# The down projection of a decoder layer by seven quarter products, with weight sums made by accumulating transfers

## The chip, the cores and the metric

The kernel runs on one core of one Trainium2 chip. A core has five engines that run side by side, each through its own list of instructions in order: TensorE (PE; its weight loads are listed as PEld), VectorE (DVE), ScalarE (ACT), GpSimd (POOL) and SyncE (SP, which here only issues transfers). Sixteen DMA engines move data between the main memory (HBM) and the on-chip memory SBUF; matmul results go to PSUM, from which DVE and ACT read them. The metric is the time of one execution on the device in microseconds (us), as the median of the runs shown. Engines wait for one another through semaphores that a framework places, from the order in which the program names the operations and from the tiles that they read and write.

## The reference

One decoder layer: two parallel token mixers (gated linear attention and sliding-window attention with sinks), merged by gates, an output projection, a layer norm, then a SwiGLU channel mixer and a second norm. There is one sequence of 512 tokens, a model width of 1024 and a channel-mixer width of 2816, all in float32. What matters here is the end:

```
def swiglu_ffn(h, w_gate, w_up, w_down):
    return (jax.nn.silu(h @ w_gate) * (h @ w_up)) @ w_down
...
        h = layer_norm(DEEPNORM_ALPHA * h + mix, ln1_g[layer], ln1_b[layer])
        ffn = swiglu_ffn(h, w_ffn_gate[layer], w_ffn_up[layer], w_ffn_down[layer])
        h = layer_norm(DEEPNORM_ALPHA * h + ffn, ln2_g[layer], ln2_b[layer])
```

The down projection is the product of the activations (512 x 2816) and `w_down` (2816 x 1024).

## The kernel before

A float32 product is made of three products of a reduced format (float32r). Every operand is split into a high part, which is the value cast to float32r, and a low part, which is the value minus the high part. High x high, low x high and high x low are then added up in one PSUM bank of 128 x 512. So each product of two tiles is three matmuls, and each operand costs a cast on ACT and a subtraction on DVE or POOL.

The weights are streamed. `plan` (L103) lists units of 128 x 1024 floats (512 KB); `fetch_to` (L141) has SP load them into three rotating buffers `raw`; `prep_to` (L149) casts a unit on ACT to `wh` (L161) and subtracts on DVE to `wl` (L162), five rotating buffers of each; `weight` (L166) hands out the parts and prepares three units ahead of use. `feat_tile` (L222) multiplies one 128-column weight tile with the whole of a transposed activation, 24 matmuls for eight k-tiles (L230).

The stages follow in the order of the text: the input projections with both mixers woven in between, branch products and gates (from L672), the merge, the output projection with tokens on partitions (L756 for the first half of the columns, L767 for the second), the first norm (`norm_part` L713, `norm_end` L718), a transposition (`transpose_in` L206), SwiGLU (from L773), the down projection (from L800) and the second norm. In SwiGLU each of 22 feature tiles f takes a gate product, an up product and `swiglu` (L776): a sigmoid on ACT (L778), two multiplications on DVE (L779, L780), then the split of the activation, a cast to `ah` on ACT (L783) and a subtraction to `al` on POOL (L784).

The down projection holds 22 k-tiles of `ah` and `al` and streams `w_down` in 22 units. The first 512 columns are finished for all four token tiles in four PSUM banks, then the second 512. For the last eight k-tiles of the second half the loop goes by token tile, so that the norm of one token tile runs beside the matmuls of the next; the last token tile is cut into two halves of 256 columns. `down` (L803) issues the three matmuls (L807). `norm_part` adds the residual and takes statistics (L715, L716). `norm_end` centres on DVE (L727), refines the root and then scales and shifts, either on DVE (L739) or, for the columns that `aside` names, on ACT (L742) and POOL (L743). SP and ACT store the two halves of each row (L834, L835).

Residual tiles and the gains of the norms are loaded from POOL's queue (L710, L704). All of SBUF's tiles come from one pool: 44 rotating tiles `hold`, 12 `scratch`, two `big` ones for the transposed activations, and the weights' buffers. PSUM has four banks `mm` and four `at`. A scheduler sets each engine's list from the program's order and from when it expects operands to be ready; `tc.issue_after` puts an instruction behind a named one.

## Time and profile before

| what | value |
|---|---|
| runs | 878.52, 881.78 and 878.04 us; median 878.52 |
| the profiled execution's span | 876.6 us, mean clock 0.995; its own time has 1.9 us more, if it stood at the median |
| PE busy | 854.8 us of the span |
| DVE, ACT, POOL busy | 448.8, 319.7, 127.3 us |
| moved by DMA | 83.03 MB, 95 GB/s in the mean |
| the down projection, from SwiGLU's last matmul to its own last | about 746 to 867 us of the span |

The head of the page gives each engine's busy time; its slices cut the span into forty parts and give the busy share of each part in tenths, with the clock that PE was granted. The groups of instructions give, for one line, engine and shape, how many there were, their busy time, the mean length of one in ns, and the idle time ahead of them with what ended it. The chain of waits follows the work that ended last back to its releasers (start, length, engine, tile, line, number). The order of time lists single instructions with start and length. A table of stretches gives, for a window, its length, the busy time of PE, PEld, DVE, ACT and POOL with the number of their instructions, then PE's clock, the share of the DMA engines and GB/s.

### The profile page before, as it was taken

The numbers are of one execution on the slowest core, as the hardware profiler recorded it, in microseconds if no ns is written. First come the engines' busy times: TensorE is split into PE (matmuls) and PEld (weight loads), VectorE is DVE, ScalarE is ACT, GpSimd is POOL, SyncE is SP. The second block draws the span as 40 slices with busy tenths as digits, with TensorE's granted clock in tenths as the row PEclk, the third lists the DMA queues.
The fourth block names the chain that finished last, engine by engine and source line by source line (L and its number), as shares of the span: only waits on it lengthen the run. The fifth ranks groups of instructions, "written<-read, shape, count | busy, mean of one in ns | idle before, by whom it ended". The sixth has DMA issues, their size and how long they took to land.

```text
span 876.6 us, 10823 instructions
## 1 busy us (share of the span) xinstructions
PE 854.8 (98%) x4226; PEld 710.2 (81%) x4226; DVE 448.8 (51%) x850; ACT 319.7 (36%) x570; POOL 127.3 (15%) x126
## 2 busy tenths in 40 slices
PE   6999999999999999999998999999999999999995
PEld 6887777777887888888887898888888888888885
DVE  4898887686676533322454854333333333224227
ACT  4557566464543431122343133333332222211111
POOL 3240220112310230000231001111111111000001
PEclk9999999999999999999999999999999999999998
DMA  8423113122122223322228103333333332322402
GB/s 241 145 72 96 49 49 97 49 72 74 49 74 71 96 96 96 96 95 97 96 91 293 49 9 113 96 96 97 97 96 97 100 99 98 125 100 79 143 0 97
DMA packets 69443, 83.03 MB, mean 95 GB/s; under 512 B 4128, under 2 KB 56368, under 8 KB 69392
## 3 DMA queue, kind: packets, MB, share of 16 engines
q1 hardware_dynamic: 67248, 76.88, 27.5%
q0 software_dynamic: 1568, 4.40, 1.5%
q10 hardware_dynamic: 576, 1.05, 0.3%
q8 instruction: 33, 0.54, 0.2%
q14 instruction: 18, 0.15, 0.1%
HBM read 80.23 MB, written 2.10 MB: 94 GB/s over the span
## 4 chain that ended last, share of the span: by engine, by line
PE 83%; issue 13%; DMA 2%; POOL 1%; ACT 0%; DVE 0%; SPq 0%; POOLq 0%; ACTq 0%; DVEq 0%
PE pg L230 12%; PE pu L230 12%; PE pva L424 5%; PE pq L230 5%; PE pr L230 5%; PE pgb L230 5%; PE pbb L230 5%; PE pba L230 5%; PE pga L230 5%; PE pw L767 3%; PE pka L230 3%; PE pqa L230 2%; PE pw L756 2%; PE po L405 2%; PE pp L394 2%
## 5 line engine op out<-in xcount | busy, mean ns | idle before, releaser
L162 DVE TENSOR_TENSOR wl<-raw,wh 128x1024 fp32r<-128x1024 f32 (+1 forms) x144 | 176.7, 1231 | 216.7 <-ACT wh L161 216.2
L161 ACT CAST wh<-raw 128x1024 fp32r<-128x1024 f32 (+1 forms) x144 | 147.1, 1027 | 236.2 <-PE pdn L807 74.8
L807 PE MATMUL pdn<-wh,al 128*128 128x512 f32 (+1 forms) x198 | 72.5, 366 | 0.0
L807 PE MATMUL pdn<-wh,ah 128*128 128x512 f32 (+1 forms) x198 | 72.4, 366 | 0.0
L807 PE MATMUL pdn<-wl,ah 128*128 128x512 f32 (+1 forms) x198 | 71.9, 365 | 0.0
L784 POOL TENSOR_TENSOR al<-sg,ah 128x512 fp32r<-128x512 f32 x22 | 33.2, 1509 | 249.1 <-ACT ah L783 249.1
L230 PE MATMUL pg<-h1h,wh 128*128 128x512 f32 x160 | 62.3, 389 | 0.0
L230 PE MATMUL pg<-h1l,wh 128*128 128x512 f32 x160 | 62.3, 389 | 0.0
L230 PE MATMUL pg<-h1h,wl 128*128 128x512 f32 x160 | 62.2, 389 | 0.0
L230 PE MATMUL pu<-h1h,wh 128*128 128x512 f32 x160 | 62.2, 389 | 0.0
L230 PE MATMUL pu<-h1l,wh 128*128 128x512 f32 x160 | 62.2, 389 | 0.0
L230 PE MATMUL pu<-h1h,wl 128*128 128x512 f32 x160 | 62.2, 389 | 0.0
L807 PEld LDWEIGHTS pdn<-wh,ah 128*128 128x128 f32 x198 | 37.4, 189 | 6.3
L807 PEld LDWEIGHTS pdn<-wh,al 128*128 128x128 f32 x198 | 37.4, 189 | 6.1
L807 PEld LDWEIGHTS pdn<-wl,ah 128*128 128x128 f32 x198 | 37.3, 188 | 6.1
L780 DVE TENSOR_TENSOR sg<-pu,sg 128x512 f32<-128x512 f32 x20 | 13.8, 692 | 46.8 <-PE pu L230 46.8
L230 PEld LDWEIGHTS pg<-h1l,wh 128*128 128x128 f32 x160 | 30.1, 188 | 6.3
L230 PEld LDWEIGHTS pg<-h1h,wl 128*128 128x128 f32 x160 | 30.1, 188 | 6.3
L230 PEld LDWEIGHTS pu<-h1h,wl 128*128 128x128 f32 x160 | 30.0, 188 | 6.3
L230 PEld LDWEIGHTS pu<-h1l,wh 128*128 128x128 f32 x160 | 30.0, 188 | 6.2
L230 PEld LDWEIGHTS pu<-h1h,wh 128*128 128x128 f32 x160 | 30.1, 188 | 6.1
L230 PEld LDWEIGHTS pg<-h1h,wh 128*128 128x128 f32 x160 | 30.0, 188 | 6.1
(423 smaller groups left out, 1942.3 us busy)
## 6 DMA issues: line engine op xcount, KB each, us to landing
raw<-in_w_in_dram SPq DMA_DIRECT2D x50, 512.0 KB, 3.4
raw<-in_w_ffn_gate_dram SPq DMA_DIRECT2D x22, 512.0 KB, 3.5
raw<-in_w_ffn_up_dram SPq DMA_DIRECT2D x22, 512.0 KB, 3.5
raw<-in_w_ffn_down_dram SPq DMA_DIRECT2D x22, 512.0 KB, 3.2
raw<-in_w_branch_b_dram SPq DMA_DIRECT2D x8, 512.0 KB, 3.3
raw<-in_w_branch_a_dram SPq DMA_DIRECT2D x8, 512.0 KB, 3.4
raw<-in_w_out_dram SPq DMA_DIRECT2D x8, 512.0 KB, 3.2
x<-in_x_dram SPq DMA_DIRECT2D x8, 256.0 KB, 6.6
```

Of the source, the lines that this page charges most:

```text
L161: ACT.copy(wh, src)
L162: DVE.tensor_tensor(wl, src, wh.bitcast(F32), ALU.subtract)
L230: PE.matmul(ps[:, n0:n1], w, d[k][:, n0:n1] if isinstance(d, list) else d[:, k, n0:n1], start=i == 0, stop=i == 3 * NK - 1)
L394: PE.transpose(pt[:, h * P : (h + 1) * P], S[h][:, n * P : (n + 1) * P], ident)
L405: PE.matmul(po[par * HD : (par + 1) * HD, 0:2, :], vtok[:, blk * P + kv * HD : blk * P + (kv + 1) * HD], PT[n][:, par::2, :], start=n == 0 ...
L424: PE.matmul(pa[c], d[:, k, cs], w, start=k == 0 and i == 0, stop=k == NK - 1 and i == 2)
L756: PE.matmul(pw[t], d[k][:, ts], w, start=k == 0 and i == 0, stop=k == NK - 1 and i == 2)
L767: PE.matmul(ps, d[k][:, ts], w, start=n == 0, stop=n == 3 * NK - 1)
L780: DVE.tensor_tensor(sg, pu, sg, ALU.mult)
L784: POOL.tensor_tensor(tl, sg, th.bitcast(F32), ALU.subtract)
L807: PE.matmul(ps[:, c0:c1], d[k][:, ts], w[:, c0:c1], start=start and n == 0, stop=stop and n == 2)
```

## The change

Both operands of the down projection are cut into quarters: the activations into A11, A12 (tokens 0 to 255, first and second eleven k-tiles) and A21, A22 (tokens 256 to 511), the weights into B11, B12 (first eleven k-tiles; first and second 512 columns) and B21, B22. The eight quarter products are replaced by seven products of quarters and of sums of quarters:

| product | PSUM | left operand | right operand |
|---|---|---|---|
| 1 | X | A11 | B11 |
| 2 | Y | S1 = A21 - A22 | T1 = B11 + B12 |
| 3 | X, added to | S2 = S1 - A11 | T2 = T1 + B22 |
| 4 | W | A22 | T4 = T2 + B21 |
| 5 | Z | A12 | B21 |
| 6 | X, added to | A11 - A21 | T3 = B12 + B22 |
| 7 | Y, added to | S4 = A12 + S2 | B22 |

Products 2, 3 and 4 are interleaved by pairs of k-tiles, each a step behind the one before. Each of X, Y, W and Z is two banks, for two token tiles. As partial results are complete, DVE adds or subtracts them into the residual tiles.

The sums of the activations are made by DVE, pair by pair, in tiles `ssum`. The sums of the weights are made in the `raw` tiles by transfers that add to what they find there, issued from POOL's queue. The activations are kept in float32 after SwiGLU and are split when a product needs them. The weights of this stage are no longer in `plan` and are split by a function of their own.

The one SBUF pool becomes several that follow each other in the same memory: `xparts` (then `merged`, then `operands`) on one side, `early` and `mix` (then `late`, with `h1` and then `sums` behind it) on the other. A tile of a new pool waits for the users of the tiles that lay there. The residual and gain tiles, the second half of the output weights and the activations lie in `late`; the output weights' second half is split in whole units of 1024 columns.

The diff, cut to its core (the pools' renamings and the unchanged parts are left out):

```
-    for j in range(2):
-        plan(("dn", j), rows(w_ffn_down[0], 0, NF, 512 * j))
...
-                parts = [(hold(f"wh{i}_{n}", F32R), hold(f"wl{i}_{n}", F32R), raw[:, 512 * n : 512 * n + 512])
-                         for n in range(2)]
+                parts = [(four(f"wh{i}", F32R), four(f"wl{i}", F32R), raw)]
...
+    right.release()
+    right = phase("merged", "right")
...
+    mix.release()
+    early.release()
+    late = phase("late")
...
     def swiglu(f, pg, pu):
+        a = act[f // HF][f % HF // 2][:, f % HF % 2, :]
         sg = scratch(f"sg{f}")
         ACT.activation(sg, pg, AF.Sigmoid)
         DVE.tensor_tensor(sg, pg, sg, ALU.mult)
-        DVE.tensor_tensor(sg, pu, sg, ALU.mult)
-        new = hold if f < 18 else scratch
-        th, tl = new(f"ah{f}", F32R), new(f"al{f}", F32R)
-        ACT.copy(th, sg)
-        POOL.tensor_tensor(tl, sg, th.bitcast(F32), ALU.subtract)
-        ah.append(th)
-        al.append(tl)
+        DVE.tensor_tensor(a, pu, sg, ALU.mult)
...
+    def load(name, p, src):
+        home, bufs = (wpool, NRAW) if name in ("b11", "b21") else (top, 7)
+        raw = home.tile([P, 1024], F32, tag="raw", name=f"raw{name}{p}", bufs=bufs)
+        nc.sync.dma_start(raw.rearrange("p (k c) -> p k c", c=512)[:, : n_of(p)], src)
+        return raw
+
+    def add(raw, p, src):
+        nc.gpsimd.dma_start(raw.rearrange("p (k c) -> p k c", c=512)[:, : n_of(p)], src, accum_op=ALU.add)
+
+    def split_w(name, p, raw):
+        n = 512 * n_of(p)
+        wh, wl = [wpool.tile([P, 1024], F32R, tag=t, name=f"{t}{name}{p}", bufs=5) for t in ("wh", "wl")]
+        ACT.copy(wh[:, :n], raw[:, :n])
+        DVE.tensor_tensor(wl[:, :n], raw[:, :n], wh[:, :n].bitcast(F32), ALU.subtract)
+        return wh, wl
+
+    def split_a(name, p, src):
+        op = right.tile([P, 2, 2, 256], F32R, tag="op", name=f"op{name}{p}", bufs=8)
+        n = n_of(p)
+        ACT.copy(op[:, 0, :n], src[:, :n])
+        POOL.tensor_tensor(op[:, 1, :n], src[:, :n], op[:, 0, :n].bitcast(F32), ALU.subtract)
+        return op
...
+    def terms(ps, op, w, p, t, start, stop, c0=0, c1=512):
+        todo = [(j, x, y) for j in range(n_of(p)) for x, y in ((0, 0), (1, 0), (0, 1))]
+        for i, (j, x, y) in enumerate(todo):
+            PE.matmul(ps[:, c0:c1], op[:, x, j, t * P : (t + 1) * P], w[y][:, 512 * j + c0 : 512 * j + c1],
+                      start=start and i == 0, stop=stop and i == len(todo) - 1, skip_group_check=True)
...
+    b11 = [load("b11", p, quarter(0, 0, p)) for p in range(3)]
+    traw = {}
+    for p in range(NP_):
+        if p >= NP_ - 3:
+            q = p - (NP_ - 3)
+            traw[q] = load("t", q, quarter(0, 0, q))
+            if q >= 1:
+                add(traw[q - 1], q - 1, quarter(0, 1, q - 1))
+        if p + 3 < NP_:
+            b11.append(load("b11", p + 3, quarter(0, 0, p + 3)))
+        both(X, op_a11(p), split_w("b11", p, b11[p]), p, p == 0, p == last)
...
+    for s in range(NP_ + 2):
+        if s + 3 < NP_:
+            traw[s + 3] = load("t", s + 3, quarter(0, 0, s + 3))
+        if 2 <= s + 2 < NP_:
+            add(traw[s + 2], s + 2, quarter(0, 1, s + 2))
+        if s >= NP_ - 1:
+            q = s - (NP_ - 1)
+            b21[q] = load("b21", q, quarter(1, 0, q))
+        if s < NP_:
+            w1, o1 = split_w("t1", s, traw[s]), op_s1(s)
+            add(traw[s], s, quarter(1, 1, s))
+            both(Y, o1, w1, s, s == 0, s == last)
+        if 0 <= s - 1 < NP_:
+            p = s - 1
+            w2, o2 = split_w("t2", p, traw[p]), op_s2(p)
+            add(traw[p], p, quarter(1, 0, p))
+            both(X, o2, w2, p, False, p == last)
+        if 0 <= s - 2 < NP_:
+            p = s - 2
+            both(W, op_a22(p), split_w("t4", p, traw[p]), p, p == 0, p == last)
...
+    for p in range(NP_):
+        if p + 3 < NP_:
+            b21[p + 3] = load("b21", p + 3, quarter(1, 0, p + 3))
+        if p >= 1:
+            t3[p - 1] = load("t3", p - 1, quarter(0, 1, p - 1))
+        if p >= 2:
+            add(t3[p - 2], p - 2, quarter(1, 1, p - 2))
+        both(Z, op_a12(p), split_w("b21", p, b21[p]), p, p == 0, p == last)
...
+    for p in range(NP_):
+        if p + 5 < NP_:
+            t3[p + 5] = load("t3", p + 5, quarter(0, 1, p + 5))
+        if p + 4 < NP_:
+            add(t3[p + 4], p + 4, quarter(1, 1, p + 4))
+        if p >= 2:
+            b22[p - 2] = load("b22", p - 2, quarter(1, 1, p - 2))
+        both(X, op_s3(p), split_w("t3", p, t3[p]), p, False, p == last)
...
+    for p in range(4, NP_):
+        b22[p] = load("b22", p, quarter(1, 1, p))
+    early_ = 2
+    for p in range(early_):
+        both(Y, op_s4(p), split_w("b22", p, b22[p]), p, False, False)
+    ops = [op_s4(p) for p in range(early_, NP_)]
+    ws = [split_w("b22", p, b22[p]) for p in range(early_, NP_)]
+    for t in range(2):
+        norm_end(2 + t, st2[2 + t][:, 0:2, :], g2, b2, "b", (512, 512))
+        store(2 + t)
+    scaled = None
+    for t in range(2):
+        spans = [(0, 512)] if t == 0 else [(0, 256), (256, 512)]
+        for n, (c0, c1) in enumerate(spans):
+            for p in range(early_, NP_):
+                terms(Y[t], ops[p - early_], ws[p - early_], p, t, False, p == last, c0, c1)
+            with tc.issue_after(scaled.ins) if n else nullcontext():
+                norm_part(Y[t], t, 1, st2[t], 1 + n, c0, c1, first=False)
+        scaled = norm_end(t, st2[t][:, 0 : 1 + len(spans), :], g2, b2, "b", (0, 0) if t == 0 else (256, 0), t == 1)
+        store(t)
```

A quarter has eleven k-tiles, so six pairs p, the last with one tile (`n_of`). `both` calls `terms` for the two token tiles of a half.

More of the change, by code (lines that the diff above doesn't have):

```diff
@@ L698, in tile_decoder_layer, with two, scratch @@
             ml.append(tl)
+    mix.release()
+    early.release()
+    late = phase("late")
+    def two(name, tag, bufs, dt=F32):
+        return late.tile([P, 512], dt, tag=tag, name=name, bufs=bufs)
+    def scratch(name, dt=F32):
+        return two(name, "scratch", 4, dt)
     def vec_bcast(v, name):
-        ts = [hold(f"{name}{i}") for i in range(2)]
+        ts = [two(f"{name}{i}", "gain", 4) for i in range(2)]
         for i in range(2):
@@ L705, in vec_bcast @@
         return ts
-    res = [[hold(f"res{t}_{i}") for i in range(2)] for t in range(NT)]
+    res = [[two(f"res{t}_{i}", "res", 8) for i in range(2)] for t in range(NT)]
     for t in range(NT):
@@ L798, in tile_decoder_layer @@
         swiglu(f, pg, pu)
+    right.release()
+    right = phase("operands", "right")
+    top.release()
+    top = phase("sums")
+    ssum = [top.tile([P, 2, 256], F32, tag=f"ssum{p}", name=f"ssum{p}") for p in range(NP_)]
     g2, b2 = vec_bcast(ln2_g, "g2"), vec_bcast(ln2_b, "b2")
     st2 = new_stats("b")
-    def down(k, t, ps, w, start, stop, c0=0, c1=512):
-        ts = slice(t * P, (t + 1) * P)
-        h, l = w
-        for n, (d, w) in enumerate(((ah, h), (al, h), (ah, l))):
-            PE.matmul(ps[:, c0:c1], d[k][:, ts], w[:, c0:c1], start=start and n == 0, stop=stop and n == 2)
@@ L824, in tile_decoder_layer @@
-    last = [weight(("dn", 1), k, 0, 512) for k in range(split, NF)]
-    aside = [(0, 0), (0, 0), (512, 512), (256, 0)]
-    scaled = None
-    for t in range(NT):
-        for n, (ps, span) in enumerate(zip(pw[t], spans[t])):
-            for k in range(split, NF):
-                down(k, t, ps, last[k - split], False, k == NF - 1, *span)
-            with tc.issue_after(scaled.ins) if n else nullcontext():
-                norm_part(ps, t, 1, st2[t], 1 + n, *span)
-        scaled = norm_end(t, st2[t][:, 0 : 1 + len(spans[t]), :], g2, b2, "b", aside[t], t == NT - 1)
+    wd_rows = w_ffn_down[0].rearrange("(k p) c -> p k c", p=P)
@@ new lines, in tile_decoder_layer @@
+    last = NP_ - 1
+    b11 = [load("b11", p, quarter(0, 0, p)) for p in range(3)]
[10 more added lines that the diff above has]
+    for t in range(2):
+        r = res[t][0]
+        DVE.scalar_tensor_tensor(r, r, ALPHA, X[t], ALU.mult, ALU.add)
@@ new lines, in tile_decoder_layer @@
+    for t in range(2):
+        r = res[t][1]
+        DVE.scalar_tensor_tensor(r, r, ALPHA, X[t], ALU.mult, ALU.subtract)
+        for i, ps in ((0, W), (1, Y)):
+            r = res[2 + t][i]
+            DVE.scalar_tensor_tensor(r, r, ALPHA, ps[t], ALU.mult, ALU.add)
+    for p in range(NP_):
[6 more added lines that the diff above has]
+        both(Z, op_a12(p), split_w("b21", p, b21[p]), p, p == 0, p == last)
```

109 lines of the change are left out of this document (77 added, 32 removed).

## The prediction, made before the change was run

> **What bounds the kernel now.** I read the head of the page first, then its slices.
>
> ```profile
> span 876.6 us, 10823 instructions
> PE 854.8 (98%) x4226; PEld 710.2 (81%) x4226; DVE 448.8 (51%) x850; ACT 319.7 (36%) x570; POOL 127.3 (15%) x126
> PE   6999999999999999999998999999999999999995
> PEclk9999999999999999999999999999999999999998
> DMA  8423113122122223322228103333333332322402
> GB/s 241 145 72 96 49 49 97 49 72 74 49 74 71 96 96 96 96 95 97 96 91 293 49 9 113 96 96 97 97 96 97 100 99 98 125 100 79 143 0 97
> ```
>
> PE is busy 98% of the span at full clock, and every other engine has half its time free. The last six slices (21.9 us each) hold the down projection: PE nines until the end, DMA at four tenths or less. So only fewer matmuls, or a shorter head or tail, can gain. A busy PE is not yet PE at its pitch; the chain of waits gives that, and a table of stretches says whether the down projection has the same.
>
> ```profile
> 735.53 5.44 PE pg L230 x24
> 749.72 61.68 issue
> 752.00:792.00 40.00, 40.00 (x178) 33.15 (x177) 9.75 (x8) 8.43 (x8) 0.00 (x0) 1.00 0.27 92
> ```
>
> 24 matmuls in 5.44 us are 0.2267 us each; 178 in the 40 us of the down projection (both ends cut into one) agree. The columns after PE and its loads are DVE, ACT and POOL: there they work 24%, 21% and 0%, and the DMA engines 27%. (The chain itself shows the down projection as "issue", because it follows a gain load on POOL; so I cost this stage from PE's own rows.) The profiled execution spans 876.6 us, the median of the runs is 878.52: 1.9 us lie around the span, and I add them at the end.
>
> **What is removed.** The down projection is 22 k-tiles x 4 token tiles x 2 column halves x 3 terms = 528 matmuls of 512 columns. Seven products of 11 k-tiles x 2 token tiles x 3 terms are 462. Shapes and operand types stay, so the pitch stays: 66 x 0.2267 = 15.0 us less, and 462 x 0.2267 = 104.7 us left. A product is 15.0 us, one pair of k-tiles of one product 12 x 0.2267 = 2.72 us. That is all the change can win here; the rest is what it pays. In pairs of k-tiles a product is 5.5, seven are 38.5.
>
> **What is added on ACT, DVE and POOL.** Before, the weights of this stage were split in 22 units, and the activations in 22 inside SwiGLU. After, each of 38.5 pairs needs a weight split (ACT cast, DVE subtraction) and an activation split (ACT cast, POOL subtraction), and four operand sums of 5.5 pairs need a DVE add. Rows with these shapes, from the page and from the groups of instructions:
>
> ```profile
> L161 ACT CAST wh<-raw 128x1024 fp32r<-128x1024 f32 x136 | 142.8, 1051 | 229.6 <-PE pdn L807 74.8 <-PE pbb L230 34.2 <-PE pg L230 28.2
> L783 ACT CAST ah<-sg 128x512 fp32r<-128x512 f32 x22 | 13.6, 619 | 58.0 <-DVE sg L780 57.8 <-issue 0.2
> L693 DVE TENSOR_TENSOR gb<-gb,ga 128x512 f32<-128x512 f32 x8 | 5.5, 692 | 0.3
> L784 POOL TENSOR_TENSOR al<-sg,ah 128x512 fp32r<-128x512 f32 x22 | 33.2, 1509 | 249.1 <-ACT ah L783 249.1
> L727 DVE SCALAR_TENSOR_TENSOR res<-res,mva,g 128x512 f32<-128x512 f32 x8 | 5.9, 747 | 0.1
> L743 POOL TENSOR_TENSOR res<-res,b 128x512 f32<-128x512 f32 x2 | 2.5, 1258 | 53.3 <-ACT res L742 53.3
> ```
>
> ACT: 38.5 x (1.05 + 0.62) = 64.3 us of 104.7, covered. The casts that leave SwiGLU gain nothing: PE bounds that stage too. DVE and POOL are another matter, since POOL's 1509 ns is a mean of two cases, which the order of time shows (start, length):
>
> ```profile
> 551.51 1.23 DVE L162 TENSOR_TENSOR wl<-raw,wh 128x1024 fp32r<-128x1024 f32 x1 [0.21 <-ACT wh L161]
> 552.07 1.81 POOL L784 TENSOR_TENSOR al<-sg,ah 128x512 fp32r<-128x512 f32 x1 [9.58 <-ACT ah L783]
> 606.48 1.29 POOL L784 TENSOR_TENSOR al<-sg,ah 128x512 fp32r<-128x512 f32 x1 [9.08 <-ACT ah L783]
> 529.43 3.45 DVE L162 TENSOR_TENSOR wl<-raw,wh 128x1024 fp32r<-128x1024 f32 x2
> 530.39 1.40 POOL L784 TENSOR_TENSOR al<-sg,ah 128x512 fp32r<-128x512 f32 x1 [1.55 <-ACT ah L783]
> ```
>
> Alone POOL's subtraction takes 1.29 us. Started inside a DVE subtraction it takes 1.81 and ends 1.14 us after DVE's end (553.88 against 552.74). The other way round, two DVE subtractions with a POOL one between them take 3.45 us, and the second ends 1.09 us after POOL's (532.88 against 531.79). They take turns: a weight split and an activation split cost 1.09 + 1.14 = 2.23 us of one shared thing. For 38.5 pairs that is 85.9 us; the 22 sums at 0.69 add 15.2; the norms of token tiles 2 and 3, which fall into the last product, 4 x 0.75 on DVE and 4 x 1.26 on POOL, 8.0. Together 109.1 us against 104.7 of PE: 4.4 us over. What is done before the first matmul of the stage counts against it; the first product uses activations that are complete halfway through SwiGLU. One pair ahead is certain (2.2 us), three are likely (6.7, by the five buffers of split weights). I take one: 2.2 us lost, between nothing and 4.4. (DVE alone has 38.5 x 1.23, the 15.2, the 3.0 and 24 readings of a PSUM bank or a row of statistics at about the same 0.69: 82 us, covered.)
>
> The Trainium skill (SBUF — State Buffer, Who interferes with whom) says that a VectorE instruction with two SBUF inputs and a GpSimd instruction that reads SBUF exclude each other, the later one waiting for the whole of the earlier. The trace agrees in kind; by whole instructions the sum would be larger, which is the second rival.
>
> **What is added in transfers.** Loads: B11, the running sum's first quarter, B21, T3's first, B22: 27.5 units of 512 KB, in place of 22 units that moved the whole matrix once. Accumulating transfers: three into each of the six running sums, one into each of six T3 tiles, 24 in all, 22 units. The rows for their price:
>
> ```profile
> q1 hardware_dynamic: 67248, 76.88, 27.5%
> q0 software_dynamic: 1568, 4.40, 1.5%
> raw<-in_w_ffn_down_dram SPq DMA_DIRECT2D x22, 512.0 KB, 3.2
> res<-in_x_dram POOLq DMA_DIRECT2D x8, 256.0 KB, 7.4
> L710 POOL DMA_DIRECT2D res<-in_x_dram x8 | 4.3, 552 | 0.0
> ```
>
> 76.88 MB in 27.5% of 876.6 us of sixteen engines are 319 GB/s when busy, 1.64 us for 512 KB; POOL's queue has 335 GB/s by its row. No transfer before accumulates. Its price lies between a plain one, 1.64 us, and two, 3.28 us, since the tile is read as well as the weights; a gain is excluded, since the same bytes still arrive. I take the middle, 2.4, as it is near neither end for a reason. The Trainium skill (DMA: Bandwidth & Descriptors, Where 436 GB/s comes from) puts the ceiling at 435 GB/s; two reads of 512 KB would be 2.4 us by that, an estimate; no row here shows it.
>
> The middle of the stage is three interleaved products (Y, X, W), in steps of 3 x 2.72 = 8.16 us. A step issues one load and three accumulations: 1.64 + 3 x 2.4 = 8.84 us, 0.68 over, 3.7 us in 5.5 steps (with cheap accumulations 6.6 us: hidden). Counted over the five products after the first but the last one (74.8 us): 20.5 loads and 22 accumulations less the three and two issued in the first product, 76.7 us, 1.9 over. I take 3.7. The fence's last row gives POOL 0.55 us per issue, 13.2 us for 24: with 38.5 x 1.29 = 49.7 POOL is occupied 63 us of 104.7.
>
> **Queues behind the new waits.** POOL issues in order, so an accumulation that waits for a load holds the activation splits behind it. In the first product the earliest waits for a tile that lies where SwiGLU's inputs did: free at SwiGLU's end, landing 3.2 us later. The splits behind it, for pairs four and five, are due 4 x 2.72 = 10.9 us after that end: covered. In the middle each accumulation follows the split of the same tile and is read a step, 8.16 us, later; even 7.4 us to landing, which the eight issued together had, fits. If that cover is gone, each microsecond over shows once as a shift, and PE's idle time has a second price:
>
> ```profile
> 475.56 1.05 ACT wh L161
> 476.00:478.60 2.60, 0.00 (x0) 0.03 (x1) 2.48 (x4) 1.39 (x2) 0.00 (x0) 1.00 0.75 241
> 478.60:482.00 3.40, 3.40 (x9) 2.65 (x10) 3.40 (x6) 2.16 (x3) 0.00 (x0) 0.53 0.77 239
> ```
>
> After 2.6 us without a matmul, at the output projection, the clock was 0.53 for 3.4 us: 9 matmuls where 15 fit, another 1.4 us. Short waits spread over the steps, as I expect, keep clear of this.
>
> **Pools in phases.** The memory of a phase serves the next, tile by tile. The residual and the second half of the output weights land where branch operands lay that the merge reads last, and are needed one output half, 8 x 4 x 3 x 0.2267 = 21.8 us, later. Hidden; if not, the 2.6 us gap above grows or, as the weights come in one cast of 1.05 instead of two of 0.62, shrinks. I put it at 0, between -2 and +3.
>
> **The tail.**
>
> ```profile
> 860.04 1.41 DVE L739 SCALAR_TENSOR_TENSOR res<-res,yb,b 128x512 f32<-128x512 f32 x2
> 867.25 0.42 DVE L715 SCALAR_TENSOR_TENSOR res<-res,pdn 128x256 f32<-128x256 f32 x1 [1.23 <-PE pdn L807]
> ```
>
> Before, DVE stood idle 1.23 us for PE's last matmul, because the tile before the last left its scale and shift to ACT and POOL. Now that tile keeps them on DVE (1.41 us, the first row's pair), and its successor's matmuls are 21, not 24 (0.7 us less cover). 1.41 + 0.7 - 1.23 = 0.9 late at most, nothing if the scale and shift are put behind the last tile's statistics; I take 0.7, since the order written has them ahead.
>
> **Sum:** 876.6 - 15.0 + 3.7 + 2.2 + 0 + 0.7 = 868.2 us of span, 870.1 with what lies around it.
>
> **Rivals.** (1) The accumulations are dear. For: nothing before does them, they read what they write. Against: the DMA engines are at 27% in this stage, and the plain price leaves 13 us to spare. At 3.28 us the middle needs 20.5 x 1.64 + 22 x 3.28 - 3 x 1.64 - 2 x 3.28 = 94.3 us against 74.8: 19.5 us late, 876.6 - 15.0 + 19.5 + 0.7 + 1.9 = 883.7, slower; at 3.5 us 888. It decides from 3.0 us per 512 KB, where its delay is the 14.3 us that are won.
> (2) DVE and POOL bound the stage by turns of whole instructions: 38.5 x (1.23 + 1.29) + 15.2 + 8 = 120.2 us, 15.5 over, 8.8 to 13.3 after one to three pairs ahead; with 11, 876.6 - 15.0 + 11 + 0.7 + 1.9 = 875.2, no change to speak of. For: any wait on a cast or a landing leaves the turn unused. Against: the two turns measured above are shorter than the rows' lengths. This is the rule of the skill's page named above, taken at its word.
> (3) The new pools hold up the output projection or SwiGLU's start, by 3 us or more of waiting and clock, with the rest as forecast: 874 to 877.
>
> **How the numbers follow.** Forecast 0.55, at 864 to 874; rival 1 0.21, rival 2 0.17, rival 3 0.07. A measurement of this kernel tells 0.5%, 4.4 us, from no change: faster is below 874.1, slower above 882.9. Faster: the forecast and a little of rival 3, 0.57. Slower: rival 1 and little else, 0.22. The rest, 0.21, lies between. Range: nothing lost, 876.6 - 15.0 + 1.9 = 863.5, is the low end; the high end is 886, within rival 1, beyond which about 0.12 lies. The forecast's own range is 864 to 874.
>
> **What would show it.** Right: 462 matmuls in the down projection at 0.2267 us, gaps of under a microsecond before pairs of the middle, DVE and POOL subtractions end on end, accumulations of 2 to 3 us of sixteen engines. Rival 1: ACT's casts there wait for POOL's transfers, the DMA row at nines, the clock dipping. Rival 2: PE waits on POOL's splits with the DMA engines half idle. Rival 3: PE's gaps before SwiGLU. Wrong altogether: PE's pitch changed, or a tail over 11 us.

## The result and the profile after

| | before | after |
|---|---|---|
| median of four runs | 879.0 us (878.04 to 881.78) | 906.59 us (904.05 to 909.47) |
| span of the profiled execution | 876.6 us | 902.3 us |
| the down projection, from its first matmul's start to its last one's end | 121.0 us | 137.0 us |
| the tail, from PE's last matmul to the end | 9.43 us | 14.36 us |

The change makes the kernel slower: ratio 1.0316, 95% interval 1.0285 to 1.0347. The forecast was 870.1 us, the range ended at 886. First the head of the page after, with its slices (22.6 us each):

```profile
span 902.3 us, 10790 instructions
PE 857.2 (95%) x4115; PEld 699.6 (78%) x4115; DVE 515.9 (57%) x896; ACT 345.4 (38%) x608; POOL 188.7 (21%) x172
PE   7999999999999999999999999999999999497993
PEclk9999999999999999999999999999999999799997
DMA  8423113131222223333356133333333338999532
```

PE's row of nines, unbroken before, has a 4 and a 7 in the down projection. With the 4 the clock falls to 7 tenths, and the DMA row stands at 8 and 9 for four slices, where it had 2 to 4. 25.7 us of span are to be found: 4.7 are gone before SwiGLU (its first matmul starts at 508.6 us, before at 503.9), 16.0 in the down projection, 4.9 in the tail.

In the down projection 462 matmuls are left, as predicted, but PE waits and then runs slowly. The waits of the profile after, from 745 to 890 us: engine, tile and line, what it waited for, then total, times and longest.

```profile
ACT wht L858 <- DMA rawt<-in_w_ffn_down_dram: 31.9, 10, 7.1
...
PE dny L879 <- DVE wlt L859: 6.2, 1, 6.2
...
PE dnx L879 <- ACT wht L858: 5.1, 1, 5.1
PE dnw L879 <- ACT wht L858: 4.5, 2, 2.5
```

PE waits for split weights, and the casts that make them wait for transfers. PE's gaps in this stage are 19.6 us. Around them the clock is at half in four stretches, 20.5 us in all. Of these 5.2 us lie in the gaps themselves; the other 15.3 us do half the work, so 7.6 us are lost to the clock. The stretch with the two longest gaps, in the table of stretches (39 matmuls in 26 us at a clock of 0.74, DMA engines at 0.95):

```profile
766.00:792.00 26.00, 13.36 (x39) 9.68 (x38) 15.81 (x13) 6.89 (x8) 15.53 (x14) 0.74 0.95 188
```

The transfers that add, by the groups and the issues of the page after:

```profile
L853 POOL DMA_DIRECT2D rawt<-in_w_ffn_down_dram x24 | 30.7, 1361 | 21.0 <-DMA rawt<-in_w_ffn_down_dram 12.5
...
rawt<-in_w_ffn_down_dram POOLq DMA_DIRECT2D x20, 512.0 KB, 9.2
```

And their queue from 750 to 880 us (packets, MB, share of sixteen engines):

```profile
q0 software_dynamic: 6016, 11.54, 50.7%
```

0.507 x 130 us are 65.9 us of sixteen engines for 22 units: 3.0 us for 512 KB, where 2.4 was forecast, and 9.2 us from issue to landing. A packet of 2 KB takes 184 ns; plain ones on SP's queue take 100. POOL needs 1.36 us to issue one, not 0.55.

The pitch changed too. Two groups of the chain of waits:

```profile
277.00 5.60 PE pgb L233 x24
840.02 10.98 PE dnz L879 x47
```

5.60 us for 24 matmuls are 0.2333 each (before: 5.47 in the same place, 0.228), and 10.98 for 47 are 0.2336. SwiGLU kept 0.2267. For 462 matmuls the longer pitch is 3.0 us. Together, -15.0 + 19.6 + 7.6 + 3.0 = 15.2 us, an estimate from these numbers, accounts for most of the 16.0 us that the stage is longer. Last, the tail: DVE in order of time around PE's last matmul, which ends at 888.0:

```profile
887.06 1.23 DVE L501 TENSOR_TENSOR yb<-yb,wb 128x1 f32<-128x1 f32 x1
890.33 0.41 DVE L740 TENSOR_TENSOR res<-res,dny 128x256 f32<-128x256 f32 x1
890.66 2.16 DVE L764 SCALAR_TENSOR_TENSOR res<-res,yb,b 128x512 f32<-128x512 f32 x2
892.75 0.41 DVE L741 BATCH_NORM_STATS2 bnb<-res 128x6 f32<-128x256 f32 x1
```

DVE takes the last sum 2.3 us after PE's end, because norms of earlier tiles are still in its list (an operation on one column, 0.15 us elsewhere, takes 1.23 here), and puts the scale and shift of tile 0 ahead of the last statistics, as the prediction read it from the order.

### The profile page after: what moved, and what is told of

Same layout as the page of the kernel before. It is cut to its first block, busy times and chain, and to the rows that moved or that the text cites. A ratio compares the mean times of both kernels' runs of the same rounds, so it can differ in the third digit from the quotient of the medians.

```text
span 902.3 us, 10790 instructions
## 1 busy us (share of the span) xinstructions
PE 857.2 (95%) x4115; PEld 699.6 (78%) x4115; DVE 515.9 (57%) x896; ACT 345.4 (38%) x608; POOL 188.7 (21%) x172
## 4 chain that ended last, share of the span: by engine, by line
PE 84%; DMA 7%; POOL 3%; issue 2%; DVE 2%; ACT 1%; SPq 0%; POOLq 0%; ACTq 0%; DVEq 0%
PE pg L233 12%; PE pu L233 12%; PE pgb L233 5%; PE pva L427 5%; PE pq L233 5%; PE pga L233 5%; PE pr L233 5%; PE pba L233 5%; PE pbb L233 5%; DMA rawt<-in_w_ffn_down_dram 5%; PE pw L791 3%; PE pka L233 2%; PE pqa L233 2%; PE po L408 2%; PE dnx L879 2%
## 5 line engine op out<-in xcount | busy, mean ns | idle before, releaser
L165 DVE TENSOR_TENSOR wl<-raw,wh 128x1024 fp32r<-128x1024 f32 x118 | 147.9, 1255 | 150.0 <-ACT wh L164 149.8
L164 ACT CAST wh<-raw 128x1024 fp32r<-128x1024 f32 x118 | 123.5, 1050 | 210.8 <-PE pg L233 75.3
L866 POOL TENSOR_TENSOR ops<-ssum,ops 128x512 fp32r<-128x512 f32 (+1 forms) x18 | 33.6, 1999 | 128.3 <-ACT ops L865 128.2
L866 POOL TENSOR_TENSOR opa<-act,opa 128x512 fp32r<-128x512 f32 (+1 forms) x18 | 29.6, 1698 | 108.4 <-ACT opa L865 108.4
L859 DVE TENSOR_TENSOR wlt<-rawt,wht 128x1024 fp32r<-128x1024 f32 (+1 forms) x24 | 36.5, 1539 | 20.8 <-ACT wht L858 20.8
L808 DVE TENSOR_TENSOR act<-pu,sg 128x512 f32<-128x512 f32 x20 | 13.8, 691 | 47.4 <-PE pu L233 47.4
L858 ACT CAST wht<-rawt 128x1024 fp32r<-128x1024 f32 (+1 forms) x24 | 23.2, 976 | 36.8 <-DMA rawt<-in_w_ffn_down_dram 31.9
L807 DVE TENSOR_TENSOR sg<-pg,sg 128x512 f32<-128x512 f32 x20 | 13.7, 687 | 39.2 <-ACT sg L806 39.2
L701 POOL TENSOR_TENSOR ml<-gb,mh 128x512 fp32r<-128x512 f32 x8 | 11.1, 1389 | 119.7 <-ACT mh L700 119.7
L853 POOL DMA_DIRECT2D rawt<-in_w_ffn_down_dram x24 | 30.7, 1361 | 21.0 <-DMA rawt<-in_w_ffn_down_dram 12.5
```

Source lines behind the costliest of these rows:

```text
L164: ACT.copy(wh, src)
L165: DVE.tensor_tensor(wl, src, wh.bitcast(F32), ALU.subtract)
L808: DVE.tensor_tensor(a, pu, sg, ALU.mult)
L853: nc.gpsimd.dma_start(raw.rearrange("p (k c) -> p k c", c=512)[:, : n_of(p)], src, accum_op=ALU.add)
L858: ACT.copy(wh[:, :n], raw[:, :n])
L859: DVE.tensor_tensor(wl[:, :n], raw[:, :n], wh[:, :n].bitcast(F32), ALU.subtract)
```

## The experiments

Three theories stand at first. *Transfers*: the accumulations are too slow, or too late, for a use one step later. *Turns*: DVE and POOL block each other. *Place*: the new pools put operands where PE reads them more slowly. All times are medians; each ratio is to the kernel before, run on the same chip. The median of the kernel before lay between 877.8 and 879.9 us from one series of runs to the next, so a difference between runs of two series is good to about 2 us.

| run | what it is | us | ratio, 95% interval |
|---|---|---|---|
| e1_aligned | change, right-hand pools moved by 32 bytes | 899.26 | 1.0228 [1.0207, 1.0250] |
| e2_plain | change, transfers do not add | 888.48 | 1.0116 [1.0077, 1.0155] |
| e3_no_low | change, POOL's subtractions left out | 909.09 | 1.0336 [1.0309, 1.0362] |
| e4_plain_no_low | both of these | 888.51 | 1.0107 [1.0081, 1.0133] |
| e5_early_sums | e1, eight of 24 accumulations inside SwiGLU | 893.94 | 1.0169 [1.0149, 1.0188] |
| e6_early_sums_tail | e5, tile 0's shift on ACT and POOL | 892.52 | 1.0149 [1.0129, 1.0170] |
| e7_early_plain | e5, transfers do not add | 883.69 | 1.0038 [1.0023, 1.0052] |
| e8_before_shift | before, inputs of SwiGLU and mixers moved by 32 bytes | 890.24 | 1.0122 [1.0101, 1.0143] |
| e9_spread | e6, another order of products | 881.44 | 1.0042 [1.0028, 1.0057] |
| e10_spread_z | e9, product 5 whole in the middle | 883.72 | 1.0063 [1.0046, 1.0079] |
| e11_spread_no_low | e9, POOL's subtractions left out | 866.48 | 0.9873 [0.9851, 0.9895] |
| e12_spread_plain | e9, transfers do not add | 877.11 | 0.9980 [0.9964, 0.9997] |
| e13_inplace | e9, work moved into SwiGLU | 882.44 | 1.0036 [1.0019, 1.0052] |
| e14_inplace_tail | e13, more matmuls for the last tile | 883.33 | 1.0048 [1.0032, 1.0065] |
| e15_spread_dve | e9, DVE subtracts in place of POOL | 871.58 | 0.9911 [0.9890, 0.9932] |
| e16_inplace_dve | e13, DVE subtracts in place of POOL | 869.26 | 0.9882 [0.9857, 0.9907] |
| e17_aligned_dve | e1, DVE subtracts in place of POOL | 902.23 | 1.0274 [1.0240, 1.0309] |
| e18_early_dve | e6, DVE subtracts in place of POOL | 889.16 | 1.0120 [1.0089, 1.0150] |

**Place.** In the change the tiles on the right-hand side start 32 bytes off a multiple of 64.

```
+    spare = phase("spare", "right")
+    gap = spare.tile([P, 8], F32, tag="gap", name="gap")
+    nc.gpsimd.memset(gap, 0.0)
     right = phase("xparts", "right")
```

> The changed kernel with a spare tile of 32 bytes per partition ahead of the pools on the right side, so that every tile there starts at a multiple of 64 bytes instead of 32 beyond one. Nothing else differs. Theory (place): in the changed kernel's trace the 512-column matmuls that read a tile of the right side start 233.3 ns apart, all others 227; the start address is the cause. Expected: 227 ns for all of them, SwiGLU's first matmul 4.7 us earlier (504 us of the span instead of 508.6), and the whole 5 to 9 us shorter, about 899. Rival (order): the scheduler's other order of the mixers costs the 4.7 us; then the pitch stays at 233 and the time at 906.

7.3 us less. The 512-column matmuls start 227 to 228 ns apart in every stage (medians), and SwiGLU starts at 503.4 us. The profiled executions differ by 5.2 us, all of it ahead of SwiGLU: the down projection takes 136.9 us, where the change took 137.0, so what the pitch gives back there is lost again; the gaps are longer (21.0 us). The counter-test moves two of before's tiles off by the same 32 bytes:

```
+    bigs = ctx.enter_context(tc.tile_pool(name="bigs", bufs=1))
+    gaps = [bigs.tile([P, 8], F32, tag="gap0", name="gap0")]
...
     def big(name):
-        return pool.tile([P, NK, T], F32R, tag="big", name=name, bufs=2)
+        t = bigs.tile([P, NK, T], F32R, tag="big", name=name, bufs=2)
```

> The kernel before with its two large tiles (transposed inputs, then transposed norm outputs) moved by 32 bytes, from a multiple of 64 to 32 beyond one; nothing else is moved by an odd 32. Theory (place): about 2270 matmuls of 512 columns read them, each 6.4 ns longer: 14.5 us slower, 893 to 895, and a pitch of 233 ns in SwiGLU too. Rival: the side of the memory or the pools' order is the cause, then 879 to 880 and 227 ns.

10.3 us more, and the pitch of SwiGLU goes from 0.2267 to 0.2333 us, as the chain of waits of the shifted kernel shows (14.5 us were expected; in the profiled executions SwiGLU's end is 12.3 us later and the span 12.1 us longer):

```profile
568.35 5.60 PE pg L238 x24
```

**Transfers.** The accumulations become plain transfers on the same queue, so the sums of the weights are left out.

```
-        nc.gpsimd.dma_start(raw..., src, accum_op=ALU.add)
+        nc.gpsimd.dma_start(raw..., src)
```

> The changed kernel with the 24 transfers from POOL's queue writing instead of adding (the weight sums are left out, so later products use single quarters). Bytes, queues, waits and all other work stay. Theory (dear accumulations): a 2 KB packet takes 184 ns where it adds and 100 where it does not, 3.0 against 1.6 us of sixteen engines per 512 KB, and that is what PE waits for in the three interleaved products (19 us of gaps, and about 10 us at half clock after them). Expected: packets of 100 ns, gaps under 5 us, no half clock before the end, about 20 to 27 us less: 880 to 886. Rival (turns): DVE and POOL set the pace of the stage; then no more than 4 us less, 902 or more.

18.1 us less than the change, a little short of what was expected. From 750 to 880 us, the queue's share and the time to landing, then the group of POOL's issues:

```profile
q0 software_dynamic: 3200, 11.54, 26.5%
...
rawt<-in_w_ffn_down_dram POOLq DMA_DIRECT2D x20, 512.0 KB, 5.7
```

```profile
L853 POOL DMA_DIRECT2D rawt<-in_w_ffn_down_dram x24 | 16.7, 697 | 14.6 <-DMA rawt<-in_w_ffn_down_dram 8.2 <-DVE wlt L859 5.1 <-PE dnx L879 0.8
```

The same 11.54 MB take 34.5 us of sixteen engines, not 65.9, and land in 5.7 us, not 9.2; the stage's gaps fall from 19.6 us to 10.0, its time at half clock from 20.5 to 3.4. The edit also changes the packets: the same bytes went in 5632 packets of 2 KB and now go in 2816 of 4 KB (each count in the view has 384 of 4 bytes beside them), so "packets of 100 ns" didn't come, a plain one of 4 KB took 195. SP's plain packets of 2 KB take 100 ns, 1.6 us for 512 KB as well, so the packets' size alone is not the price. The transfers are the largest part of the loss in this order of work.

**Turns, first try.** POOL's subtractions are left out: low part times weights is missing, the high part is used twice, so PE's work stays.

```
-        POOL.tensor_tensor(op[:, 1, :n], src[:, :n], op[:, 0, :n].bitcast(F32), ALU.subtract)
...
-        todo = [(j, x, y) for j in range(n_of(p)) for x, y in ((0, 0), (1, 0), (0, 1))]
+        todo = [(j, x, y) for j in range(n_of(p)) for x, y in ((0, 0), (0, 0), (0, 1))]
```

> The changed kernel without POOL's 42 subtractions in the down projection; the matmuls that took a low part of the activations take the high part again, so their number is the same and the low x high terms are left out. Theory (dear accumulations): the gaps of the middle stay, 15 us or more; only the last two products and the tail gain, where DVE is busy without a break: 4 to 8 us less, 899 to 903. Rival (turns): the gaps of the middle go with POOL's subtractions, 20 us or more less, 887 or under.

> Both edits at once: transfers that write instead of adding, and no POOL subtractions (sums and low x high terms are left out). What is left is 462 matmuls at 233 ns, the head that is 4.7 us late, and the tail. Theory (dear accumulations, and turns at the end): 872 to 878, PE without gaps over 1 us in the down projection, a tail of about 10 us after the last matmul. Rival: if a gap of several microseconds stays at the start of the second product, the memory that SwiGLU frees too late, or the latency of the first sums, is a cause of its own.

No gain in either. In the first, DVE's subtractions are back at 1.22 us, but PE's wait only moved (waits of PE, 745 to 890 us):

```profile
PE dnx L878 <- ACT wht L858: 12.3, 1, 12.3
```

So in the change's own order the turns lie beside waits for transfers. Taken alone this seems to refute the turns; e11 will show that it does not. In e4, expected at 872 to 878, a wait of PE of 5.0 us for a cast of weights is left in product 3, with 6.8 us of half clock around it, and that cast waits for a landing. So the rival of its expectation holds in kind: a landing can come too late even where the transfers do not add.

**Earlier sums.** With the aligned start, T1 and two of six T3 tiles are summed inside SwiGLU, in eight weight-sum tiles on the right-hand side.

```
+        sum_step(f - 4)
...
+    for p, tag, bufs in ((2, "op", 5), (0, "op0", 2), (1, "op0", 2)):
+        held[p] = top.tile([P, 2, 2, 256], F32R, tag=tag, name=f"opa11{p}", bufs=bufs)
```

> The aligned version with the first weight sums made earlier: the tiles of the weight sums change places with the split activations (right side, free during SwiGLU, eight tiles), so that all six T1 and the first two T3 are loaded and added during SwiGLU, where the DMA engines are under a third busy. All arithmetic is the changed kernel's. Theory (dear and late accumulations): the 14.2 us of gaps at the start of the second product and the half clock behind them (17 us, worth 8.5) go, the 16 units of accumulation that are left fit beside the later products: about 879 (875 to 884), in place of the aligned version's 899. Rival (throughput): what is left, 3 us for each 512 KB, still starves PE in the three interleaved products: gaps of 8 us or more between the second and the fifth product, 888 or more.

> As the version with early sums, and the scale and shift of the token tile before the last goes to ACT and POOL instead of DVE. Theory (tail): the 2.2 us of that scale and shift stand on DVE between the last tile's sum and its statistics; without them the span ends 2 us sooner. Rival: POOL's additions of three token tiles then queue up (1.26 us each, six of them) and the end is no sooner, or later by 1 to 2 us.

> The version with early sums, its 24 transfers writing instead of adding (the weight sums are left out). If accumulations no longer bound anything, the same time as with early sums, within 2 us. If they still do, the difference is their price in place: 5 us or more.

5.3 us for the earlier sums, far less than expected, and 1.4 for the tail; and the price of the accumulations is still 10 us (e7 against e5). The likely reason is that T2 and T4 are still read one step after they are asked for; the next edit asks that.

**Another order.** `e9` interleaves product 2 with product 1, product 3 with the beginning of product 5 and with product 4, and leaves the rest of product 5 behind product 6. Two A11 operands are split inside SwiGLU. `e10` does all of product 5 in the middle.

```
+    prod1(0)
+    for p in range(NP_):
+        if p + 1 < NP_:
+            prod1(p + 1)
...
+        prod2(p)
...
+    for n, p in [(i[0], int(i[1])) for i in "x0 x1 z0 x2 z1 x3 w0 x4 w1 x5 w2 w3 w4 w5".split()]:
+        (prod3 if n == "x" else prod4 if n == "w" else prod5)(p)
...
+    for p in (2, 3, 4, 5):
+        prod5(p)
```

> Starts from the version with the early sums and the aligned start. New order of the same 38.5 pairs: product 2 is interleaved with product 1, product 3 with the beginning of product 5 and with product 4, so that every running sum is read two to three pairs of other products (11 to 16 us) after its accumulating transfer is asked for instead of one step (8.16 us); the rest of product 5 comes after product 6, so that the norms of token tiles 2 and 3 lie beside 24 us of matmuls and not beside 15; the first two A11 operands are split inside SwiGLU. If the waits in the middle come from the time to landing (9.2 us) and not from the sixteen engines' time, the down projection has less than 3 us of gaps and no half clock, about 109 us in place of 117 to 121; and if the tail is long because DVE has the norms of three token tiles behind PE's last matmul, it falls from 13.9 to 10 or 11 us. Together 874 to 881 us. If the throughput of the accumulating transfers is what is short (66 us of sixteen engines at 3.0 us per 512 KB, spread as thinly as this), the gaps stay and it is 888 or more.

> As the version before it, but all of product 5 is done in the middle and product 6 is followed at once by product 7, as in the change. The middle has even more between a sum's request and its use, so it should be free of waits as well. If the tail's length is DVE's backlog of norms, it is back at 13.5 to 14.5 us after PE's last matmul, 3 to 4 us more than in the other order, and the time is that much longer; if the tail comes from something else (the stores, the last matmuls being fewer), both have the same tail.

11.1 us less than e6: later use helps, though not quite to the 874 to 881 of the expectation. Gaps of 2.3 and 3.0 us stay, with a half clock behind each. The tail is 13.2 us in e9 and 13.9 in e10 (13.9 in e6), so the place of the norms is not most of it. What holds it now was asked by leaving out either suspect, as in e3 and e2:

> The version with the spread order, with POOL's 42 subtractions of the activations left out (the low part times the high part of the weights is left out of the result; the high part is multiplied twice instead, so PE's work is the same). In the change itself this gained nothing, since the accumulating transfers were late anyway. In the spread order DVE is busy 14 to 15 of every 15 us from 825 to 870 us. If DVE and POOL taking turns is what holds it now, DVE's subtractions go back to 1.2 us, the gaps of the middle shrink to under 3 us and the tail falls from 13.2 to 10 us: 871 to 876 us. If the turns still lie beside other waits, it stays within 2 us of 881.4.

> The version with the spread order, with the accumulating transfers replaced by plain ones of the same bytes on the same queue (the sums of the weights are left out of the result). If the accumulating transfers still hold it, the two waits in the middle and their half clock (about 8.7 us together) are gone: 872 to 875 us. If the turns of DVE and POOL hold it, the gaps only move to other pairs and it stays at 878 to 882.

Now POOL's subtractions are worth 15.0 us, more than expected, and the accumulations 4.3. The same stretch of both, first e9, then e11 (PE, PEld, DVE, ACT, POOL):

```profile
750.00:825.00 75.00, 69.23 (x287) 55.16 (x286) 68.28 (x50) 37.96 (x54) 50.93 (x42) 0.95 0.80 172
```

```profile
750.00:825.00 75.00, 75.00 (x332) 62.10 (x331) 48.32 (x57) 44.05 (x61) 17.03 (x15) 1.00 0.86 199
```

With POOL's work gone DVE gets 57 instructions done in 48.3 us where it had 50 in 68.3, and PE never waits. Is it the sum of the work, as the prediction costed it? `e13` moves work into SwiGLU and leaves nothing out: S1 in place of A21, five A11 operands split there; S3 becomes -(S2 + A22). `e14` gives the last token tile 27 matmuls of cover instead of 21.

```
+            s = act[0][p][:, :, HIH]
+            DVE.tensor_tensor(s, s, act[1][p][:, :, HIH], ALU.subtract)
...
+        DVE.scalar_tensor_tensor(s3[:, :n], quad(0, HIH, p)[:, :n], -1.0, s3[:, :n], ALU.mult, ALU.subtract)
...
-    early_ = 2
+    early_ = 1
```

> The version with the spread order, and nothing left out. Work of DVE and POOL is moved out of the down projection, not removed: the sums S1 of five of six pairs (3.5 us of DVE) are made inside SwiGLU, in place of A21, and five of the six A11 operands are split there (three more than before it, 3.4 us of turns), in memory that the first norm's gains and an unused half tile leave; S3 is made from S2 and A22. If the spread order is held by the sum of DVE's and POOL's turns, 6.9 us of them less in the stage take 4 to 8 us off: 873 to 878 us, at or a little below the kernel before. If it is the order of single waits that holds it (an accumulating transfer behind a late split), the two gaps in the middle stay and it is 879 to 882.

> The same with one pair of the last product, not two, done ahead for both token tiles, so that the last token tile has 27 matmuls (6.1 us) beside the norm of the tile before it instead of 21 (4.8 us). If that cover is what the tail lacks, it is 1.0 to 1.4 us shorter than in the kernel beside it; if DVE is still behind when the last product starts, the same.

Neither gained. e13 lies just above what the second theory of its expectation gave, and the cover in e14 is worth nothing. The gaps did not stay in place, though: PE has a new one of 6.3 us at 807.9 us. What was moved out came back as waiting. This is e13 in the stretch of the two rows above, and in the 28 us behind it:

```profile
750.00:825.00 75.00, 66.15 (x275) 52.21 (x274) 71.20 (x46) 35.00 (x50) 51.62 (x46) 0.95 0.81 179
825.00:853.00 28.00, 27.66 (x122) 22.35 (x121) 28.00 (x28) 16.74 (x23) 17.64 (x12) 1.00 0.30 87
```

The time for which a started DVE instruction is kept out counts as busy here, and with it DVE has hardly any time left. Over the whole down projection it is busy for 110.8 of 118.0 us in e9 and 114.0 of 119.8 in e13, against 73.8 of 106.0 in e11. So 6.9 us of work less and no time won does not rule the sum out: DVE's own work and the time that it is kept out fill the stage. Nor is the test clean. e13 brings the loads of the second norm's gains into the stage, 3.6 us of issues on POOL, and its sums in place wait for POOL's readings of the same tile, one of them for 2.9 us just ahead of the new gap. How DVE is kept out the order of time of e13 shows, some 5 us behind that gap, DVE first, then POOL in the same stretch:

```profile
818.90 10.24 DVE L891 TENSOR_TENSOR wlt<-rawt,wht 128x1024 fp32r<-128x1024 f32 x2
```

```profile
818.70 1.75 POOL L899 TENSOR_TENSOR ops<-act,ops 128x512 fp32r<-128x512 f32 x1
819.95 1.37 POOL L829 DMA_DIRECT2D rawt<-in_w_ffn_down_dram  x1
820.57 4.57 POOL L899 TENSOR_TENSOR ops<-act,ops 128x512 fp32r<-128x512 f32 x3
824.32 2.48 POOL L899 TENSOR_TENSOR ops<-act_odd,ops 128x256 fp32r<-128x256 f32 x1
825.59 2.45 POOL L899 TENSOR_TENSOR opa<-act,opa 128x512 fp32r<-128x512 f32 x1
```

Two weight subtractions of 1.22 us take 10.24. POOL has its list ready and works end on end, and the first of DVE's two ends 7.3 us after its start, 1.1 us after the fourth of POOL's subtractions. They do not take turns one for one. It is in the change as well, a sum of 0.69 us of DVE and POOL beside it:

```profile
762.76 4.25 DVE L871 TENSOR_TENSOR ssum<-act,ssum 128x512 f32<-128x512 f32 x1 [1.81 <-POOL ops L866]
```

```profile
762.39 1.49 POOL L853 DMA_DIRECT2D rawt<-in_w_ffn_down_dram  x1
763.17 3.28 POOL L866 TENSOR_TENSOR ops<-ssum,ops 128x512 fp32r<-128x512 f32 x2
```

The sum ends 0.56 us after POOL's second subtraction (767.01 against 766.45). So the last edit gives POOL's subtractions to DVE, in e9 alone and in e13, there with the scale and shift of tiles 2 and 3:

```
-        POOL.tensor_tensor(op[:, 1, :n], src[:, :n], op[:, 0, :n].bitcast(F32), ALU.subtract)
+        DVE.tensor_tensor(op[:, 1, :n], src[:, :n], op[:, 0, :n].bitcast(F32), ALU.subtract)
```

> The version with the spread order, nothing left out, and one edit: inside the down projection the low parts of the activations are subtracted by DVE instead of POOL. In the version before it DVE's weight subtractions, 1.2 us when nothing disturbs them, took 2.9 to 4.6 us wherever POOL had several subtractions end on end. If POOL's runs keep a waiting DVE instruction out to their end (not turn by turn), each POOL subtraction costs DVE more than the 0.69 us that DVE needs to do it itself: the gaps of the middle shrink to about 4 us in all, the tail to 11 or 12 us, 871 to 876 us. If they take fair turns at 2.23 us a pair, as the prediction had it, DVE's 1.92 us a pair change little, and it stays at 877 to 881.

> The same edit on the version that moves S1 and five A11 operands into SwiGLU, and the scale and shift of token tiles 2 and 3 on DVE as well (0.74 us for each half tile, where POOL's addition took 1.2 to 1.5 and kept DVE out). If POOL's runs were the cause, what is moved out of the stage now counts too: 868 to 873 us. If the sum of the turns was the cause, it is no better than 877.

9.9 us less than e9, and 13.2 less than e13: both are faster than the kernel before, by 0.9 and 1.2%, with intervals that end below 1. The move also shortens the work by the prediction's own prices, since a POOL subtraction was put at 1.14 us of the shared time and takes 0.68 on DVE. So these two runs show that waiting for POOL was the cost, and do not tell the sum of the waits from their order. By the groups of e9, then of e15, from 750 to 880 us:

```profile
L881 DVE TENSOR_TENSOR wlt<-rawt,wht 128x1024 fp32r<-128x1024 f32 x19 | 33.2, 1761 | 0.0
L881 DVE TENSOR_TENSOR wlb<-rawb,whb 128x1024 fp32r<-128x1024 f32 x12 | 24.3, 2035 | 0.0
```

```profile
L881 DVE TENSOR_TENSOR wlt<-rawt,wht 128x1024 fp32r<-128x1024 f32 x19 | 23.2, 1221 | 4.6 <-ACT wht L880 4.6
L881 DVE TENSOR_TENSOR wlb<-rawb,whb 128x1024 fp32r<-128x1024 f32 x12 | 14.6, 1214 | 3.1 <-ACT whb L880 3.1
L888 DVE TENSOR_TENSOR ops<-ssum,ops 128x512 fp32r<-128x512 f32 x15 | 10.3, 684 | 0.0
```

DVE does its own 1.2 us in 1.2 us, and POOL's subtraction in 0.68. e16, the best version that leaves nothing out, shows the stage as the prediction drew it: the stretch that answers to before's row, its chain of waits through the last products, and the head of its page.

```profile
752.00:792.00 40.00, 40.00 (x178) 33.10 (x178) 34.85 (x48) 21.80 (x29) 12.90 (x13) 1.00 0.96 220
```

```profile
802.54 9.52 PE dnw L912 x42
812.07 14.96 PE dnx L912 x66
827.02 9.52 PE dnz L912 x42
836.54 12.65 PE dny L912 x65
```

```profile
span 865.3 us, 10769 instructions
PE 840.4 (97%) x4115; PEld 696.6 (81%) x4115; DVE 504.1 (58%) x935; ACT 344.1 (40%) x606; POOL 132.3 (15%) x134
```

178 matmuls in 40 us again, with DVE at 87% and the DMA engines at 96%; PE ends the stage 106.5 us after it began, 14.5 less than before. Last: what does that edit bring without the other order?

> The change with the aligned start, nothing else moved, and the activations' low parts subtracted by DVE inside the down projection. If POOL's runs were already the larger part of the change's own loss, the 24 us of gaps and 24 us of half clock fall by more than half: 880 to 888 us, from 899. If in the change's own order the accumulating transfers are late whatever POOL does (leaving POOL's subtractions out gained nothing there), it stays at 896 to 901.

> The version with the early sums and the change's order of products, with the same edit; 892.5 us with POOL's subtractions. If the spread order matters by itself, this stays well above 871.6, at 880 to 886; if the early sums and DVE's subtractions are all that was needed, it comes to 872 to 876.

Little: 3.0 us more in the change's order, 3.4 less with the early sums, against 9.9 in the new one. PE's waits in e17 and e18 (from 745 us on):

```profile
PE dnx L882 <- ACT wht L861: 12.9, 1, 12.9
PE dnw L882 <- ACT wht L861: 9.0, 2, 7.1
```

```profile
PE dnw L898 <- ACT opa L884: 5.5, 1, 5.5
PE dnx L898 <- DVE opa L885: 4.3, 1, 4.3
```

In e17 accumulations take 10.7 us to landing, and the casts wait for them. e18 and e15 move the same bytes by the same queues; the 17.6 us between them come from the order and from the two A11 operands split inside SwiGLU, whose missing shows as the 4.3 us and a half clock behind. Two limits lie on top of each other: with the transfers late, taking POOL's subtractions away showed nothing (e3, e4) or little (e17, e18).

## Why the prediction was wrong

**The matmuls.** Right in number, 462; the 15.0 us are there to be won: e16's stage is 14.5 us shorter. What failed is "Shapes and operand types stay, so the pitch stays". In the mixers, the output projection and the down projection the pitch was 0.233: 4.7 us ahead of SwiGLU, and 3.0 in the down projection by the estimate above. Mended alone it brought 7.3 us (e1). The step on the pools, "I put it at 0", looked at waits for memory and not at where tiles start; rival 3 gave the right place and the wrong mechanism. A changed pitch and a tail over 11 us were the two signs that the prediction had named for "wrong altogether"; both came.

**The accumulations.** This is the step with the largest error: "I take the middle, 2.4". Measured: 3.0 us of sixteen engines for 512 KB, the very point from which rival 1 was to decide. The step "even 7.4 us to landing, which the eight issued together had, fits" failed with it: 9.2 us do not fit a step of 8.16. And "short waits spread over the steps" were gaps of up to 6.2 us, with four stretches of half clock that lost 7.6 us. In place, adding costs 18.1 us (e2); the forecast had 3.7. Rival 1 at 883.7 named the mechanism, and without the pitch's 7.3 us the change is still at 899.3, as its sum had neither the second price of the gaps in it nor more than 0.7 us of the tail.

**DVE and POOL.** "They take turns: a weight split and an activation split cost 1.09 + 1.14 = 2.23 us of one shared thing" was read from single meetings. As a mean price it was not far off: DVE's busy time in the stage is 37 us longer in e9 than in e11, for 40 subtractions of POOL, 0.9 us each, an estimate from the two profiles. What failed is the sum of 109.1 us and the 2.2 us lost by it. The sum left out DVE's 24 readings of PSUM and statistics, 16.6 us at the prediction's 0.69, as work of DVE alone and covered; but DVE works through its list in order, and while one instruction is kept out they wait too, as DVE's rows of e9 and e13, almost without a pause, let one conclude. And the waits are uneven: with lists ready on POOL a DVE instruction is kept out for several POOL instructions and comes late where PE needs it. Leaving POOL's subtractions out is worth 15.0 us (e11); which of the two has the larger part is open. The Trainium skill (SBUF — State Buffer, Who interferes with whom) says that the later one waits for the whole of the earlier; the trace agrees, and adds that the wait can go on over what POOL has behind it. In one place of e13 DVE did come in between two subtractions (780.76 to 784.96 us); what decides that is open. Rival 2, whole instructions in turn, at 875.2, had the right pair of engines, but not the runs of several.

**The tail.** 0.7 us was forecast, 4.9 came. DVE takes the last sum 2.3 us late, behind norms that wait for POOL; tile 0's scale and shift ahead of the last statistics, which were named, add 2.2; and 1.4 more than before lie between DVE's last instruction and the end of the span; between these some 1.0 us is saved. In e16 the tail is 12.2 us, 2.8 over before, and the 1.4 us at the very end are the same. The last long piece there is POOL's closing drain, 5.27 us in the change and in e16, 3.31 before; what makes it longer was not tried.

**The sum.** With another order, another engine for the subtractions and an aligned start the kernel runs at 869.3 us. That this is near the forecast of 870.1 is luck: it is another kernel, whose stage loses almost nothing where 5.9 us were forecast, and whose tail is 2.8 us longer where 0.7 were.

## What to carry to other kernels

An algorithm that saves matmuls is paid for in operands: ask of each new transfer not only what it moves but how long before its use it can be asked for, and let another product lie between. When removing one suspect gains nothing, another limit may lie beside it: test it again once that one is gone. Where DVE is busy, try the subtractions of POOL on DVE too: here the same work on DVE cost less time than the waiting.

## What the runs showed of the hardware that was not expected

- A tile that starts 32 bytes off a multiple of 64 makes each 512-column matmul that reads it start 0.233 us after the last, not 0.227, as the streamed operand (SwiGLU in e8) and as the loaded one (the down projection of the change, against e1).
- A 2 KB packet that adds takes 184 ns, a plain one on SP's queue 100 ns; POOL's plain transfers of the same bytes went in packets of 4 KB, of 195 ns (e2). POOL issues a transfer of 512 KB that adds in 1.36 us beside other work, a plain one in 0.70.
- A DVE instruction with two SBUF operands of 1.22 us waits while POOL works through a list: two of them took 10.24 us together (e13).
- Around gaps of 2.0 to 6.2 us in the change PE ran at half clock for 3.4 to 10.2 us, in part inside the gap; in e2 gaps of 2.4 and 2.6 us passed without.
